# A decoder layer on one core: Silu as one activation, and elementwise work moved from GpSimd to VectorE

## The chip, the cores and the metric

The kernel runs on one core of one Trainium2 chip. A core has a tensor engine (PE in the profile), a vector engine (DVE), a scalar engine (ACT), GpSimd (POOL) and SyncE (SP), which here only starts transfers. Each engine takes its instructions in order and waits on semaphores for what others make. The metric is the device time of one execution in microseconds; lower is better.

## The reference

One decoder layer over 512 tokens of width 1024, in float32:

```python
h = layer_norm(x, ln_in_g, ln_in_b)
proj = h @ w_in
pool_in, qkv, z, beta_raw, a_raw, gate_a, gate_b = split(proj)
y_a = multiscale_pool(pool_in, pool_w, pool_scale)   # trailing means over 2, 4, 8, 16 positions minus the token
y_b = gated_deltanet(qkv, z, beta_raw, a_raw, ...)   # silu(conv4(qkv)), delta rule, rms norm * silu(z)
mixed = sigmoid(gate_a) * y_a + sigmoid(gate_b) * y_b
h = layer_norm(alpha * h + mixed @ w_out, ln1_g, ln1_b)
r = alpha * h + square(relu(h @ w_up)) @ w_down
h = layer_norm(r + sigmoid(r @ ple_gate_w) * (p @ ple_proj_w), ln2_g, ln2_b)
```

The convolution is causal over 4 positions, one filter per channel, and silu(a) is a * sigmoid(a).

## The kernel before, in words

Activations are kept with features on the 128 partitions and the 512 tokens along the row. A wide product runs as three float32r passes over exact splits of both operands: `hi` holds the upper bits, `lo` the rest (`three`, L66 to L68). A weight comes in slabs of 128 x 1024 numbers: SP requests `raw`, ScalarE casts `hi` (L57), VectorE subtracts to get `lo` (L58). There are three `raw` buffers and four of each half, so a slab's cast waits until TensorE has left an older slab.

Start (L146 to L254): SP requests eight halves of x rows, then six rows of parameters into `prow` (L154, L155), then 16 columns for beta and decay, the first two slabs of the weight of k (`raw_k`, L188) and some small rows. VectorE takes statistics, GpSimd makes scale and offset, ScalarE normalises (L219), TensorE transposes into `ps_in`, ScalarE applies gain and offset to get `hf_in` (L239), and VectorE (for two blocks of eight ScalarE) makes the high part of `act` (L240), VectorE the low one (L241). The first two slabs are split in `k0_part`: VectorE casts `hi`, GpSimd subtracts `lo` in two halves (L202). TensorE runs the small product `ps_ba` and the first tile of k, block by block, as `act` comes.

Front, solver and scan (L380 to L600), four pairs of heads: for each of k, q and v of a head a product into PSUM, then `conv`: ScalarE scales the tile into `acc` (L350), VectorE adds three shifted multiples (L352), ScalarE takes the sigmoid into `sg` (L355), GpSimd multiplies (L356). The decay matrices `E` are made beside the first pair: VectorE and GpSimd multiply masks (`gs`, L320), TensorE sums them into `ps_d`, ScalarE takes the exponential (L327), GpSimd clears a triangle (L328). A solver and a scan over the chunks follow, with many small products between those of the next pair.

Trailing means (L633 to L650): TensorE makes a tile, ScalarE copies it, GpSimd adds shifted copies, one to four times for the four windows, ten in all (L640).

Gates (L676 to L720), four rounds of two tiles: `ps_z` with a sigmoid and a product on VectorE (L685) into `zs`; `ps_gb` with a sigmoid `sgb` (L692) and two products on GpSimd, by `sgb` (L693) and by the delta rule's output `onT` (L694); `ps_ga` with a sigmoid `sga` (L710), which VectorE multiplies by the lifted means (L714) and GpSimd adds to `zs` (L716); ScalarE and VectorE split the sum into `mx` (L718, L719). Between them VectorE makes the residual rows `y` (L668 to L671). In the output projection (L754 to L756) TensorE goes through four banks `ps_wo` in turn; the third one becomes free when the last `sga` has been multiplied. The feed-forward part and the last norm follow.

The order on each engine is set by a scheduler that works from modelled times when the program is built; `high_priority` puts the weight splits ahead.

## Time and profile before

| | |
|---|---|
| median of three runs | 887.84 us (886.15 to 889.31) |
| span of the profiled execution | 886.5 us; its device time is not given apart from the three runs |
| TensorE, matmuls | busy 860.3 us, 97% |
| TensorE, weight loads, beside the matmuls | 715.3 us, 81% |
| VectorE | 521.7 us, 59% |
| ScalarE | 357.5 us, 40% |
| GpSimd | 151.6 us, 17% |

The shares are means over stages with different limits, so the page is followed by views of single stretches: what TensorE waited for, busy time by stretch with the granted clock, and the instructions of an engine in order of time. In a row of the last kind the first number is the start and the second the duration; what is in brackets at its end is idle time before it and what ended that.

### The profile page before, as it was taken

What the parts mean: (1) busy time and instruction counts of PE and PEld (TensorE: products, weight loads), DVE (VectorE), ACT (ScalarE), POOL (GpSimd) and SP (SyncE); (2) the same over time, 40 slices, a digit from 0 to 9 for tenths busy, and PEclk for the clock granted to TensorE, in tenths of its full rate; (3) what the DMA queues carried; (4) which work ended last, traced back from release to release, by engine and by line L of the source; (5) the groups of instructions that cost most, each with busy time, mean ns of one, the idle gap of its engine ahead of it and who ended that gap; (6) DMA issues with size and microseconds to landing.
All of it is one profiled execution on the core that took longest, in us unless ns stands there. A gap on an engine that the chain in (4) does not pass through costs nothing.

```text
span 886.5 us, 12477 instructions
## 1 busy us (share of the span) xinstructions
PE 860.3 (97%) x4944; PEld 715.3 (81%) x4944; DVE 521.7 (59%) x991; ACT 357.5 (40%) x567; POOL 151.6 (17%) x135
## 2 busy tenths in 40 slices
PE   7999999999999999998999999999999999999994
PEld 5777888888888888886888888888888888888883
DVE  8898988769759336368366544433344443333456
ACT  4566455365544535333136444322124442222311
POOL 6182312113403031324000000000000000000034
PEclk9999999999999999999999999999999999999997
DMA  6322222222211313183215333333323323233202
GB/s 196 96 59 85 72 73 80 65 72 72 78 50 53 97 31 97 52 283 96 72 32 182 96 95 95 119 96 95 95 85 103 99 95 96 95 96 95 95 10 86
DMA packets 72427, 80.63 MB, mean 91 GB/s; under 512 B 4009, under 2 KB 64818, under 8 KB 72370
## 3 DMA queue, kind: packets, MB, share of 16 engines
q1 hardware_dynamic: 72370, 79.85, 29.6%
q8 instruction: 39, 0.64, 0.3%
q14 instruction: 18, 0.15, 0.1%
HBM read 77.74 MB, written 2.10 MB: 90 GB/s over the span
## 4 chain that ended last, share of the span: by engine, by line
PE 89%; DVE 6%; ACT 2%; POOL 1%; issue 1%; DMA 1%; SPq 0%; POOLq 0%; ACTq 0%; DVEq 0%
PE ps_dn L67 7%; PE ps_dn L68 7%; PE ps_dn L66 7%; PE ps_up L67 6%; PE ps_up L68 6%; PE ps_up L66 6%; PE ps_z L67 2%; PE ps_z L68 2%; PE ps_gb L66 2%; PE ps_gb L68 2%; PE ps_v L67 2%; PE ps_z L66 2%; PE ps_gb L67 2%; PE ps_v L68 2%; PE ps_v L66 2%; PE ps_ga L66 2%
## 5 line engine op out<-in xcount | busy, mean ns | idle before, releaser
L67 PE MATMUL ps_dn<-hid,hi_dn 128*128 128x512 f32 x256 | 99.9, 390 | 0.0
L68 PE MATMUL ps_dn<-hid,lo_dn 128*128 128x512 f32 x256 | 99.9, 390 | 0.0
L66 PE MATMUL ps_dn<-hid,hi_dn 128*128 128x512 f32 x256 | 99.7, 389 | 0.0
L58 DVE TENSOR_TENSOR lo_dn<-raw_dn,hi_dn 128x1024 fp32r<-128x1024 f32 x32 | 39.2, 1225 | 82.9 <-ACT hi_dn L57 82.9
L57 ACT CAST hi_dn<-raw_dn 128x1024 fp32r<-128x1024 f32 x32 | 33.7, 1054 | 96.8 <-PE ps_dn L67 85.2
L887 POOL TENSOR_TENSOR y<-y,rp 128x512 f32<-128x512 f32 x4 | 6.3, 1613 | 380.5 <-PE ps_pg L756 380.5
L66 PEld LDWEIGHTS ps_dn<-hid,hi_dn 128*128 128x128 f32 x256 | 48.1, 188 | 10.0
L67 PEld LDWEIGHTS ps_dn<-hid,hi_dn 128*128 128x128 f32 x256 | 48.1, 188 | 10.0
L68 PEld LDWEIGHTS ps_dn<-hid,lo_dn 128*128 128x128 f32 x256 | 48.1, 188 | 9.7
L849 DVE TENSOR_TENSOR relu<-relu 128x512 f32<-128x512 f32 x32 | 22.2, 693 | 53.3 <-ACT hid L848 53.3
L846 ACT ACTIVATE relu<-ps_up 128x512 f32<-128x512 f32 x32 | 19.0, 595 | 55.8 <-PE ps_up L68 55.8
L693 POOL TENSOR_TENSOR zs<-zs,sgb 128x512 f32<-128x512 f32 x8 | 15.0, 1875 | 88.0 <-ACT sgb L692 88.0
L850 DVE TENSOR_TENSOR hid<-relu,hid 128x512 fp32r<-128x512 f32 x32 | 22.1, 691 | 1.1
L352 DVE SCALAR_TENSOR_TENSOR acc_q<-ps_q,ccol,acc_q 128x511 f32<-128x511 f32 (+2 forms) x24 | 17.8, 742 | 6.3 <-ACT acc_q L350 6.0
L848 ACT ACTIVATE hid<-relu 128x512 fp32r<-128x512 f32 x32 | 20.3, 633 | 1.0
L451 DVE TENSOR_TENSOR sh<-sh,ya 128x120 f32<-128x120 f32 (+14 forms) x60 | 19.4, 324 | 0.7
L356 POOL TENSOR_TENSOR kq<-acc_k,sg_k 128x512 f32<-128x512 f32 x8 | 10.9, 1366 | 48.9 <-ACT sg_k L355 48.9
L58 DVE TENSOR_TENSOR lo_pg<-raw_pg,hi_pg 128x1024 fp32r<-128x1024 f32 x8 | 9.6, 1222 | 16.3 <-ACT hi_pg L57 16.3
L121 ACT ACTIVATE hf_l<-ps_l,pcol 128x128 f32<-128x128 f32 x32 | 11.9, 472 | 17.1 <-PE ps_l L116 17.1
L557 ACT ACTIVATE vn<-ps_s,cc 128x128 f32<-128x128 f32 x32 | 11.1, 367 | 18.6 <-PE ps_s L555 18.5
L352 DVE SCALAR_TENSOR_TENSOR acc_k<-ps_k,ccol,acc_k 128x511 f32<-128x511 f32 (+2 forms) x24 | 17.8, 742 | 1.3 <-ACT acc_k L350 1.2
L58 DVE TENSOR_TENSOR lo_wo<-raw_wo,hi_wo 128x1024 fp32r<-128x1024 f32 x8 | 10.8, 1354 | 13.0 <-ACT hi_wo L57 13.0
(947 smaller groups left out, 2557.0 us busy)
## 6 DMA issues: line engine op xcount, KB each, us to landing
raw_dn<-in_w_down_dram SPq DMA_DIRECT2D x32, 512.0 KB, 3.5
raw_wo<-in_w_out_dram SPq DMA_DIRECT2D x8, 512.0 KB, 4.0
raw_pg<-in_ple_gate_w_dram SPq DMA_DIRECT2D x8, 512.0 KB, 3.6
x<-in_x_dram SPq DMA_DIRECT2D x8, 256.0 KB, 5.3
y<-in_x_dram SPq DMA_DIRECT2D x4, 512.0 KB, 9.3
out_dram<-y SPq DMA_DIRECT2D x7, 256.0 KB, 2.0
raw_k<-in_w_in_dram SPq DMA_DIRECT2D x2, 512.0 KB, 4.0
raw_pp<-in_ple_proj_w_dram SPq DMA_DIRECT2D x2, 512.0 KB
```

The lines of the kernel that those rows point to most:

```text
L57: A.copy(hi, raw)
L58: V.tensor_tensor(out=lo, in0=raw, in1=hi.bitcast(F32), op=SUB)
L66: T.matmul(ps, wh, ah, start=first, stop=False)
L67: T.matmul(ps, wh, al, start=False, stop=False)
L68: T.matmul(ps, wl, ah, start=False, stop=last)
L352: marks[name + "v"] = V.scalar_tensor_tensor(out=acc[:, s:], in0=ps[:, :SEQ - s], scalar=w(3 - s), in1=acc[:, s:], op0=MULT, op1=ADD)
L451: V.tensor_tensor(out=sh[:, :, :m], in0=sh[:, :, :m], in1=ya[:, :, k:k + 1].to_broadcast([P, U8, m]), op=MULT)
L693: G.tensor_tensor(out=zs[m], in0=zs[m], in1=sg, op=MULT)
L846: A.activation(r, ps, AF.Relu)
L848: A.activation(hl[:, 0, :], r, AF.Square)
L849: V.tensor_tensor(out=r, in0=r, in1=r, op=MULT)
L850: V.tensor_tensor(out=hl[:, 1, :], in0=r, in1=hl[:, 0, :].bitcast(F32), op=SUB)
```

## The change

Five edits:

- The six parameter rows are requested by ScalarE's queue instead of SP's.
- The first two slabs: VectorE subtracts `lo`, in one instruction of 128 x 1024; `hi` of the second is cast by ScalarE, and the second split is issued behind block 2 instead of block 1.
- `conv` ends in one Silu activation; the sigmoid tile and GpSimd's product go (24 times).
- The ten adds of the trailing means go from GpSimd to VectorE.
- The 16 gate products and the eight sums go from GpSimd to VectorE; the product by `onT` now comes ahead of the one by `sgb`.

Comments and empty lines are changed too, so later line numbers are one to three lower.

```diff
     for i, v in enumerate((ln_in_g, ln_in_b, ln1_g[0], ln1_b[0], pool_scale[0])):
-        dma(out=prow[8 * i:8 * i + 8, :], in_=v.rearrange("(a b) -> a b", b=P))
-    dma(out=prow[40:41, :], in_=o_norm_w)
+        A.dma_start(out=prow[8 * i:8 * i + 8, :], in_=v.rearrange("(a b) -> a b", b=P))
+    A.dma_start(out=prow[40:41, :], in_=o_norm_w)
...
-        V.tensor_copy(hi, raw)
-        for a in range(0, 4, 2):
-            G.tensor_tensor(out=lo[:, a:a + 2, :], in0=raw[:, a:a + 2, :], in1=hi[:, a:a + 2, :].bitcast(F32), op=SUB)
+        (A.copy if i else V.tensor_copy)(hi, raw)
+        V.tensor_tensor(out=lo, in0=raw, in1=hi.bitcast(F32), op=SUB)
         return hi, lo
...
-        if kb == 1:
+        if kb == 2:
             with tc.issue_after(vec_last.ins):
                 wk0.append(k0_part(1))
...
-        sg = tpa.tile([P, SEQ], F32, tag="sg", bufs=2, name=f"sg_{name}")
-        A.activation(sg, acc, AF.Sigmoid)
-        G.tensor_tensor(out=dst, in0=acc, in1=sg, op=MULT)
+        A.activation(dst, acc, AF.Silu)
...
             for _ in range(g + 1):
-                G.tensor_tensor(out=dst[:, PAD:], in0=src[:, PAD:], in1=src[:, PAD - sh:PAD + SEQ - sh], op=ADD)
+                V.tensor_tensor(out=dst[:, PAD:], in0=src[:, PAD:], in1=src[:, PAD - sh:PAD + SEQ - sh], op=ADD)
...
-            G.tensor_tensor(out=zs[m], in0=zs[m], in1=sg, op=MULT)
-            G.tensor_tensor(out=zs[m], in0=zs[m], in1=onTs[o], op=MULT)
+            V.tensor_tensor(out=zs[m], in0=zs[m], in1=onTs[o], op=MULT)
+            V.tensor_tensor(out=zs[m], in0=zs[m], in1=sg, op=MULT)
...
-            G.tensor_tensor(out=ya, in0=ya, in1=sg, op=ADD)
+            V.tensor_tensor(out=ya, in0=ya, in1=sg, op=ADD)
```

The order on VectorE at the start, from the last statistics on; `hi_k` and `lo_k` are the two parts of the first slabs, `hf_in` and `act` the blocks of the normalised input. Before:

```order
L103 BN_AGGR mv_in<-st_in_181 128x2
L221 TENSOR_SCALAR x_115<-x_115,mv_in,rstd_in 128x512
L227 CAST hi_ba<-raw_ba 128x8x16
L200 CAST hi_k_196<-raw_k_144 128x1024
L240 CAST act<-hf_in_206 128x512
L241 TENSOR_TENSOR act<-hf_in_206,act 128x512
L240 CAST act<-hf_in_215 128x512
L241 TENSOR_TENSOR act<-hf_in_215,act 128x512
L200 CAST hi_k_219<-raw_k_146 128x1024
```

After:

```order
L103 BN_AGGR mv_in<-st_in_181 128x2
L220 TENSOR_SCALAR x_115<-x_115,mv_in,rstd_in 128x512
L226 CAST hi_ba<-raw_ba 128x8x16
L200 CAST hi_k_196<-raw_k_144 128x1024
L201 TENSOR_TENSOR lo_k_197<-raw_k_144,hi_k_196 128x1024
L239 CAST act<-hf_in_205 128x512
L240 TENSOR_TENSOR act<-hf_in_205,act 128x512
L239 CAST act<-hf_in_214 128x512
L240 TENSOR_TENSOR act<-hf_in_214,act 128x512
```

The low part of the first slab now stands on VectorE between its cast and the first block of `act`; the cast of the second slab has gone to ScalarE.

The order on VectorE ahead of the output projection, up to the last `sga`, with `y` the residual rows and `lo_wo` the low parts of the output weight's slabs; `zs_4045` and `zs_4074` are the two gate tiles before, `zs_3995` and `zs_4024` the same after. Before:

```order
L671 TENSOR_TENSOR y_3762<-y_3762,gb_in 128x1024
L670 TENSOR_TENSOR y_4240<-y_4240,gb_in 128x1024
L58 TENSOR_TENSOR lo_wo_4270<-raw_wo_4267,hi_wo_4269 128x1024
L671 TENSOR_TENSOR y_4001<-y_4001,gb_in 128x1024
L671 TENSOR_TENSOR y_4240<-y_4240,gb_in 128x1024
L58 TENSOR_TENSOR lo_wo_4276<-raw_wo_4273,hi_wo_4275 128x1024
L714 SCALAR_TENSOR_TENSOR sga_4193<-ps_lift_4195,pcol,sga_4193 128x512
L58 TENSOR_TENSOR lo_wo_4282<-raw_wo_4279,hi_wo_4281 128x1024
L719 TENSOR_TENSOR mx_4201<-zs_4045,mx_4201 128x512
L58 TENSOR_TENSOR lo_wo_4288<-raw_wo_4285,hi_wo_4287 128x1024
L714 SCALAR_TENSOR_TENSOR sga_4229<-ps_lift_4231,pcol,sga_4229 128x512
```

After:

```order
L58 TENSOR_TENSOR lo_wo_4220<-raw_wo_4217,hi_wo_4219 128x1024
L667 TENSOR_TENSOR y_4190<-y_4190,gb_in 128x1024
L668 TENSOR_TENSOR y_3951<-y_3951,gb_in 128x1024
L58 TENSOR_TENSOR lo_wo_4226<-raw_wo_4223,hi_wo_4225 128x1024
L691 TENSOR_TENSOR zs_4024<-zs_4024,sgb_4092 128x512
L668 TENSOR_TENSOR y_4190<-y_4190,gb_in 128x1024
L711 SCALAR_TENSOR_TENSOR sga_4143<-ps_lift_4145,pcol,sga_4143 128x512
L713 TENSOR_TENSOR zs_3995<-zs_3995,sga_4143 128x512
L58 TENSOR_TENSOR lo_wo_4232<-raw_wo_4229,hi_wo_4231 128x1024
L716 TENSOR_TENSOR mx_4151<-zs_3995,mx_4151 128x512
L58 TENSOR_TENSOR lo_wo_4238<-raw_wo_4235,hi_wo_4237 128x1024
L711 SCALAR_TENSOR_TENSOR sga_4179<-ps_lift_4181,pcol,sga_4179 128x512
```

One gate product and one sum now stand among VectorE's rows here; three products more stand a little earlier. The slabs of the output weight and the two `sga` keep their order among each other.

The order on ScalarE there, after; it is the same as before but for line and buffer numbers:

```order
L689 ACTIVATE sgb_4092<-ps_gb_4067 128x512
L707 ACTIVATE sga_4143<-ps_ga_4118 128x512
L57 CAST hi_wo_4231<-raw_wo_4229 128x1024
L715 CAST mx_4151<-zs_3995 128x512
L57 CAST hi_wo_4237<-raw_wo_4235 128x1024
L707 ACTIVATE sga_4179<-ps_ga_4154 128x512
```

ScalarE thus casts the sum of the sixth tile (`mx`) ahead of the fourth slab, and that one ahead of the last `sga`. Table loads on ScalarE: ten rows before, eleven after, where the one more stands at the first sigmoid of the gates (L680).

## Rows read from the trace of the kernel before

**Rows 1.** The page's first part: busy time, share of the span and instructions of each engine.

```profile
PE 860.3 (97%) x4944; PEld 715.3 (81%) x4944; DVE 521.7 (59%) x991; ACT 357.5 (40%) x567; POOL 151.6 (17%) x135
```

**Rows 2.** What TensorE waited for: total us, times, longest.

```profile
PE ps_wo L754 <- DVE sga L714: 3.5, 1, 3.5
...
PE ps_d L325 <- ACT E L327: 1.5, 1, 1.5
...
PE ps_q L66 <- DVE acc_k L352: 1.5, 2, 1.0
```

**Rows 3.** Stretches: their length, busy us of each engine with its instructions, then TensorE's granted clock, the share of the transfer engines and GB/s.

```profile
60.00:70.00 10.00, 8.47 (x39) 6.59 (x39) 9.95 (x15) 7.49 (x10) 6.84 (x7) 1.00 0.31 83
...
200.00:250.00 50.00, 50.00 (x420) 41.88 (x418) 39.37 (x127) 25.21 (x49) 17.05 (x15) 1.00 0.23 67
...
300.00:350.00 50.00, 50.00 (x335) 42.66 (x334) 23.60 (x46) 22.84 (x46) 11.15 (x8) 1.00 0.23 67
...
410.00:420.00 10.00, 6.50 (x30) 5.11 (x29) 6.98 (x10) 3.93 (x7) 3.50 (x2) 0.93 0.58 188
```

**Rows 4.** GpSimd's first split and VectorE's rows beside it, in order of time.

```profile
14.22 2.68 POOL L202 TENSOR_TENSOR lo_k<-raw_k,hi_k 128x512 fp32r<-128x512 f32 x2 [1.43 <-DVE hi_k L200]
...
13.45 0.69 DVE L200 CAST hi_k<-raw_k 128x1024 fp32r<-128x1024 f32 x1 [1.20 <-DMA raw_k<-in_w_in_dram]
14.30 1.47 DVE L240 CAST act<-hf_in 128x512 fp32r<-128x512 f32 x1 [0.16 <-ACT hf_in L239]
...
17.37 0.41 DVE L240 CAST act<-hf_in 128x512 fp32r<-128x512 f32 x1
```

**Rows 5.** TensorE in the same stretch: its first product, the last of the five that work on the first block, and one later wait.

```profile
15.92 0.60 PE L253 MATMUL ps_ba<-act,hi_ba 128*32 128x512 f32 x1 [0.94 <-DVE act L240]
...
18.45 0.63 PE L68 MATMUL ps_k<-act,lo_k 128*128 128x512 f32 x1
...
23.24 0.42 PE L254 MATMUL ps_ba<-act,hi_ba 128*32 128x512 f32 x1 [0.32 <-DVE act L241]
```

**Rows 6.** The requests of the start: the page's line for x (KB each, median us to landing), SP's queue for the first parameter row and the first slabs (start, duration), and ScalarE's first instruction.

```profile
x<-in_x_dram SPq DMA_DIRECT2D x8, 256.0 KB, 5.3
...
4.55 0.51 SPq L154 DMA_DIRECT2D prow<-in_ln_in_g_dram  x1
...
9.46 0.94 SPq L188 DMA_DIRECT2D raw_k<-in_w_in_dram  x2
...
5.65 1.28 ACT L219 ACT_TABLE_LOAD   x1 [5.65 <-DMA prow<-in_ln_in_b_dram]
```

**Rows 7.** VectorE and GpSimd between 56 and 68 us, in order of time for each.

```profile
57.14 1.25 DVE L397 TENSOR_SCALAR ssk<-ssk 128x8 f32<-128x8 f32 x1
...
59.74 0.17 DVE L400 TENSOR_SCALAR ncc<-cc 128x8 f32<-128x8 f32 x1
...
62.97 1.22 DVE L58 TENSOR_TENSOR lo_k1b<-raw_k1b,hi_k1b 128x1024 fp32r<-128x1024 f32 x1
...
65.22 2.29 DVE L58 TENSOR_TENSOR lo_q1a<-raw_q1a,hi_q1a 128x1024 fp32r<-128x1024 f32 x1
...
56.88 1.49 POOL L356 TENSOR_TENSOR kq<-acc_q,sg_q 128x512 f32<-128x512 f32 x1 [0.20 <-ACT sg_q L355]
...
61.29 1.04 POOL L320 TENSOR_TENSOR gs<-upper,glo 128x512 fp32r<-128x512 f32 x1
...
65.13 1.29 POOL L356 TENSOR_TENSOR vT<-acc_v,sg_v 128x512 f32<-128x512 f32 x1 [2.22 <-ACT sg_v L355]
```

**Rows 8.** Around the start of the output projection, in order of time for each of TensorE, ScalarE and VectorE.

```profile
411.53 0.39 PE L67 MATMUL ps_ga<-act,hi_ga3b 128*128 128x512 f32 x1
...
414.02 0.40 PE L756 MATMUL ps_wo<-hi_wo,mx 128*128 128x512 f32 x1
417.92 0.50 PE L754 MATMUL ps_wo<-hi_wo,mx 128*128 128x512 f32 x1 [3.50 <-DVE sga L714]
...
422.14 0.39 PE L756 MATMUL ps_wo<-hi_wo,mx 128*128 128x512 f32 x1
422.36 0.39 PE L754 MATMUL ps_wo<-hi_wo,mx 128*128 128x512 f32 x1
...
409.24 1.05 ACT L57 CAST hi_wo<-raw_wo 128x1024 fp32r<-128x1024 f32 x1 [1.84 <-PE ps_ga L67]
414.38 0.62 ACT L718 CAST mx<-zs 128x512 fp32r<-128x512 f32 x1 [4.09 <-POOL zs L716]
414.91 1.04 ACT L57 CAST hi_wo<-raw_wo 128x1024 fp32r<-128x1024 f32 x1
...
398.37 1.79 DVE L668 TENSOR_SCALAR y<-y,mv_in,rstd_in 128x1024 f32<-128x1024 f32 x1
...
405.68 2.31 DVE L58 TENSOR_TENSOR lo_wo<-raw_wo,hi_wo 128x1024 fp32r<-128x1024 f32 x1
```

**Rows 9.** Groups by line, engine and shape: busy us, mean ns of one | idle time of the engine before them, and what ended most of it.

```profile
L693 POOL TENSOR_TENSOR zs<-zs,sgb 128x512 f32<-128x512 f32 x8 | 15.0, 1875 | 88.0 <-ACT sgb L692 88.0
...
L640 POOL TENSOR_TENSOR pads<-pads 128x512 f32<-128x512 f32 x10 | 10.9, 1085 | 19.0 <-ACT pads L638 14.2 <-DVE sh L451 4.3
...
L849 DVE TENSOR_TENSOR relu<-relu 128x512 f32<-128x512 f32 x32 | 22.2, 693 | 53.3 <-ACT hid L848 53.3
...
L355 ACT ACTIVATE sg_v<-acc_v 128x512 f32<-128x512 f32 x8 | 5.1, 632 | 13.2 <-DVE acc_v L352 7.6 <-DVE ya L453 5.6
```

## The prediction

> **What bounds the kernel now.** I read the shares of busy time first: TensorE is busy for 860.3 of 886.5 us, VectorE for 521.7, ScalarE for 357.5, GpSimd for 151.6 [rows 1]. So an edit gains only where it takes idle or slow time from TensorE, about 26 us in all, part of it at the kernel's end, which the change leaves alone. The second view is the list of what TensorE waited for [rows 2]. One entry is large, 3.5 us for the vector engine's scaled gate `sga` at the first bank of the output projection; then come 1.5 us for the scalar engine's `E` and twice together 1.5 us for the vector engine's `acc_k`. Third, the stretches [rows 3]: in 60 to 70 us TensorE has 8.47 of 10 while VectorE has 9.95, and in 410 to 420 it has 6.50 at a granted clock of 0.93. Between 200 and 350 us TensorE is never idle, while VectorE has 39.4 and 23.6 of 50. So three places can gain: the start, 60 to 90 us, and the start of the output projection. Everywhere else the question is only whether the work that VectorE gets stays hidden.
>
> **The start.** The first half of `k`'s weight is split by GpSimd from 14.22 us for 2.68 us, and beside it VectorE's first cast of `act` takes 1.47 us; the next such cast takes 0.41 [rows 4]. TensorE's first product waits for that cast, 0.94 us, and starts at 15.92 [rows 5]. In the changed order VectorE splits this half itself ahead of the casts (1.22 us by the same form at 62.97 [rows 7]). That fits: the weight is now requested right behind x and not behind six parameter rows, which put SP's request at 9.46 instead of about 5 [rows 6], and VectorE stands idle for 1.20 us until 13.45, waiting for this weight [rows 4]. The first cast then ends at 14.30 + 0.41 = 14.71 instead of 15.77, and TensorE starts 1.06 us earlier. The wait of 0.32 us at 23.24 [rows 5] is also one for `act`, and the casts behind it come earlier by the stretch of the second split; I take it as gone: 1.38 us. The cast of the weight's second half goes to ScalarE, between blocks 0 and 1 of `act`: 1.05 us there (the same shape at 409.24 [rows 8]). Block 1 is later by that, but TensorE first has five products of block 0, which took it from 15.92 to 18.45 [rows 5], so I cost it at nothing; without that cover it is 1.05.
>
> Bounds: the early products run at the lower of two clock levels, 0.60 to 0.63 us, five of them up to 18.45 [rows 5], against 0.39 later [rows 8]; if the earlier start brings the upper level for all, that is 5 x 0.24 = 1.2 more, 2.6 in all. On the other side the weight's 1 MB now moves while the last x are in flight. These land 5.3 us after requests that end at about 4.5, so at 9.8 [rows 6]; if weight and x shared the transfer engines evenly from 5.0 on, the last x would be up to half of 4.8 us late, and the term would be -1.0. I take 1.38, the value nearest to the rows, because the requests stand in one queue behind x. The Trainium skill, "DMA: Bandwidth & Descriptors", section "Issuing engines are not separate DMA queues", says that transfers started by different engines run on the same 16 engines and interleave, and that a second issuer saves only issue time. By that rule the parameter rows gain nothing by coming from ScalarE and could at worst mix with x, which for 20 KB is nothing; the 0.51 us of an issue [rows 6] is what moves. Six issues of at most that on ScalarE end before its table load at 5.65, so they cost nothing; if they took twice that, from about 0.8 us on, they would push the first normalisation of x by about 1 us.
>
> **60 to 90 us.** The wait at `ps_d` hangs on `E`, which ScalarE computes behind a table load and the sigmoid of `acc_v`, which hangs on VectorE. VectorE is full there, and two of its instructions are stretched beside GpSimd's product `acc`*`sg`: L397 takes 1.25 us where an instruction of the same shape takes 0.17, and `lo_q1a` 2.29 where `lo_k1b` takes 1.22 [rows 7]. Without these products the chain is shorter by 1.08 + 1.07 = 2.15 us, of the 2.99 that TensorE waits there: 1.08 off the wait for `E`, the rest off the two for `acc_k`. I take 2.15. The upper bound is 2.99. The lower one is nothing: GpSimd's masks L320 stay, move up when the products go, and stop VectorE elsewhere, each 1.04 us long [rows 7]. The Trainium skill, "SBUF — State Buffer", section "Who interferes with whom", has a rule for this: a VectorE instruction with two SBUF inputs and a GpSimd one that reads SBUF exclude each other, and whichever comes second waits for the whole of the first. The trace agrees: L397 ends at 58.39, the GpSimd product at 58.37. By that rule two masks that get in the way would take 2.08 back, and the whole sum would be 6.1 instead of 8.2, about 881.8 us.
>
> Silu itself is not in the trace. It replaces a sigmoid of 0.63 us [rows 9]; if it took twice as long, the result would still come earlier, since a GpSimd product of 1.29 to 1.49 us [rows 7] is left out behind it. Table loads stay as many up to 90 us, and one is added at the first output gate: 1.28 us [rows 6] on an engine with 22.8 busy of 50 [rows 3], beside a TensorE that has 24 products of 0.23, 5.5 us, for the next bank. I cost it at nothing.
>
> **The output projection.** TensorE's third bank could follow the product of 414.02 at 414.25; it follows at 417.92, and from there on to 422.36 twelve steps take 4.44 us instead of 12 x 0.23 = 2.76, at the lower clock [rows 8]: 3.67 + 1.68 = 5.35 us lost. The last `sga` was late since ScalarE cast the fourth weight slab only at 414.91, behind the cast of a sum that GpSimd delivered late, and VectorE's rows before it were stretched beside GpSimd's gate products: four of them from 398.37 to 405.68, each about 1.05 us (2.31 where 1.22 is usual) [rows 7, 8]. With the products and sums on VectorE these 4.2 us go, against four products and one sum at 0.69 [rows 9], 3.5 us. What is late next is the slab's buffer: the third slab's cast began at 409.24, as TensorE left the previous slab; for the fourth this is the end of the product at 411.53, so 411.92 + 0.04. From there the old distance of 414.91 to 417.92 holds, 3.01 us, and TensorE starts at 414.97: 2.95 us earlier, with a wait of 0.7. After the wait of 1.53 us at 67 us the stretch shows a clock of 1.00 [rows 3], so I count the slow steps as gone as well: 2.95 + 1.68 = 4.63. Bounds: 5.35, and 0 if VectorE's added instructions keep the last `sga` where it was.
>
> **The rest.** Ten adds of the means and the 24 gate instructions bring VectorE 34 x 0.69 = 23.5 us between 205 and 418 us [rows 9]. I cost them at nothing beyond the above, for TensorE has work there throughout and VectorE's share stays under 0.93 in 200 to 250 us ((39.4 + 6.9)/50) [rows 3].
>
> **Sum.** 1.38 + 2.15 + 4.63 = 8.16 us off the profiled execution's span of 886.5, so 878.3. The median of the runs is 1.3 us above that span; 887.84 - 8.16 = 879.7 us.
>
> **Rivals.** First, the last `sga` stays late, because VectorE, now alone with rows of y, splits and gates, is the bound in 392 to 418 us. For it: what it is given there, 3.5 us, is nearly what it is spared, 4.2. Against it: the fourth slab's cast needs only TensorE and the sum before it, and that sum no longer waits for GpSimd. Then 1.38 + 2.15 = 3.5 us are left: 884.3.
>
> Second, the change does not do what it says: the stretched instructions are lengthened by something that stays, the masks and the transfers of y, and the earlier casts are limited by `hf_in`. For it: GpSimd keeps its masks in the very stretch where VectorE is full. Against it: the ends that coincide to 0.02 us. Then 0 to 2 us: about 887.
>
> Third, slower. VectorE takes its instructions in order. A gate product waits there for ScalarE's sigmoid, which waits for a full bank; GpSimd stood 88 us before these eight products [rows 9], where nobody was behind it. Behind it on VectorE stand the next weight's low parts and the scan's state updates, for which TensorE waits. If half of the 23.5 us shows up on TensorE, 11.7 - 8.2 = 3.6 us are lost: 891.4; all of it would be 903. It decides from a third on, 8.2 of 23.5. Against it: TensorE is never idle in the two stretches between 200 and 350 us now [rows 3], and in the changed order the splits of a slab stand well ahead of its products.
>
> **How the numbers follow.** Forecast 0.62, late `sga` 0.14, no effect 0.12, slower 0.12. A difference under 0.3%, 2.7 us, can't be told from no change. The first two cases are faster: 0.76; the third is the same: 0.12; the fourth slower: 0.12. With all upper bounds, 2.6 + 2.99 + 5.35 = 10.9, the time is 876.9; an unseen gain of the same kind puts the low end at 875.5. The high end, 886.5, takes in the late `sga` and the better part of no effect and leaves out the slower case.
>
> **What would show it.** Right: the first `act` cast at about 0.41 us and TensorE's first product near 14.9; L397 under 0.3 us and the wait for `E` under 0.6; in the output projection a wait for `sga` under 1 us and a clock of 1.00; TensorE without waits between 200 and 350 us. Wrong: waits for `act` or x at the start longer than now, the `ps_wo` wait still at 3 us, or new waits of TensorE for `S`, `rr` or `lo` between 200 and 400 us.

## The result and the profile after

The changed kernel takes 881.25 us (median of four runs, 880.27 to 881.79) against 887.31 us for the kernel before, run beside it (886.15 to 889.31): 6.06 us less by these medians. The ratio on record is 0.9923 with a 95% interval of 0.9904 to 0.9942 (the quotient of the two medians, 0.9932, lies in it), which is 6.8 us less, between 5.1 and 8.5. The prediction had 8.16 less and 879.7. The profiled execution has a span of 879.4 us, 7.1 under that of before.

The page's first part, as in [rows 1]:

```profile
PE 858.7 (98%) x4944; PEld 715.1 (81%) x4944; DVE 516.4 (59%) x1026; ACT 361.1 (41%) x569; POOL 63.1 (7%) x73
```

GpSimd has lost 88.5 us of its 151.6, and VectorE, with 35 instructions more, is busy for 5 us less: its stretched instructions are mostly gone. TensorE's busy time falls by only 1.6 us, so most of the gain is idle time. What TensorE waited for, as in [rows 2] (total us, times, longest), with the one entry above these:

```profile
PE ps_in L233 <- ACT x L218: 3.3, 4, 1.6
...
PE ps_d L324 <- ACT E L326: 0.7, 1, 0.7
...
PE ps_q L66 <- DVE acc_k L351: 0.5, 1, 0.5
```

The entry for `ps_wo` is gone; the wait for ScalarE's normalised x at the start has grown from 2.5 to 3.3 us. The same stretches as in [rows 3]: length, busy us of each engine with its instructions, TensorE's granted clock, the share of the transfer engines, GB/s.

```profile
60.00:70.00 10.00, 9.32 (x44) 7.47 (x43) 9.51 (x16) 7.25 (x10) 3.71 (x6) 1.00 0.36 105
...
200.00:250.00 50.00, 50.00 (x400) 42.11 (x399) 40.23 (x128) 26.07 (x48) 4.52 (x3) 1.00 0.24 67
...
300.00:350.00 50.00, 50.00 (x286) 42.52 (x285) 25.18 (x50) 22.08 (x42) 2.01 (x2) 1.00 0.23 67
...
410.00:420.00 10.00, 10.00 (x49) 8.13 (x48) 5.95 (x8) 4.18 (x6) 0.00 (x0) 1.00 0.30 105
```

To see where the time went, the starts of the same TensorE products were compared, kernel after minus kernel before, as a median over each stretch. The table gives what each stage adds to that difference, worked out from the profiled executions; negative is a gain. It holds all kernels run, so that the experiments can refer to it. The column "in all" is the difference from 450 us on, and the sum of those before it.

Each row rests on one execution of its kernel and on one of before, and executions of one program differ: those of before lie between 885.83 and 890.03 us, those of silu_back, means_back and order_only spread by 2.3 to 3.4 us, those of gates_back by 0.3. The profiled execution is 1.2 us above the median for silu_back and 2.5 above for means_back, and 1.6 below it for order_only, so the stages of these three rows are less firm than their decimals look.

| kernel | up to 30 us | wait at 67 us | wait at 80 us | 95 to 395 us | output projection | in all | median us | ratio, interval |
|---|---|---|---|---|---|---|---|---|
| after | -0.78 | -0.85 | -0.74 | +0.48 | -5.21 | -7.11 | 881.25 | 0.9923 [0.9904, 0.9942] |
| gates_back | -1.60 | -0.85 | -0.77 | -0.27 | -5.21 | -8.71 | 879.38 | 0.9901 [0.9885, 0.9917] |
| sums_back | -0.66 | -0.87 | -0.76 | +0.83 | -5.23 | -6.69 | 881.18 | 0.9922 [0.9900, 0.9944] |
| products_back | -1.51 | -0.85 | -0.78 | +0.11 | -5.22 | -8.25 | 880.19 | 0.9913 [0.9891, 0.9934] |
| silu_back | -1.07 | -0.01 | +0.02 | +1.80 | -1.28 | -0.54 | 886.71 | 0.9982 [0.9969, 0.9995] |
| means_back | +1.33 | -0.84 | -0.73 | +2.55 | -3.53 | -1.23 | 884.46 | 0.9960 [0.9945, 0.9974] |
| prow_sp | -2.46 | -0.85 | -0.74 | +0.48 | -5.22 | -8.79 | 879.66 | 0.9904 [0.9887, 0.9920] |
| prow_late | -0.01 | -0.85 | -0.77 | +0.51 | -5.23 | -6.34 | 882.14 | 0.9932 [0.9908, 0.9956] |
| split_back | -0.11 | -0.85 | -0.77 | +0.51 | -5.22 | -6.45 | 882.09 | 0.9934 [0.9909, 0.9960] |
| order_only | -0.11 | 0.00 | -0.80 | 0.00 | -4.55 | -5.46 | 884.66 | 0.9962 [0.9948, 0.9976] |
| gates_alone | +0.49 | -0.01 | -0.02 | +1.72 | -4.55 | -2.36 | 885.90 | 0.9969 [0.9959, 0.9979] |
| gates_back_old | +0.68 | -0.85 | -0.78 | -0.27 | -3.73 | -4.95 | 882.30 | 0.9934 [0.9919, 0.9948] |
| best | -1.79 | -0.85 | -0.78 | -0.27 | -5.21 | -8.89 | 879.25 | 0.9898 [0.9884, 0.9913] |

From 420 us to the end no kernel's difference moves by more than 0.02 us.

**The start after.** The requests (start, duration), on SP's queue and then on ScalarE's, VectorE's last statistics of x, and ScalarE's last normalisation of x:

```profile
0.79 5.78 SPq L148 DMA_DIRECT2D x<-in_x_dram  x8
...
7.09 1.75 SPq L188 DMA_DIRECT2D raw_k<-in_w_in_dram  x2
...
0.79 0.58 ACTq L154 DMA_DIRECT2D prow<-in_ln_in_g_dram  x1
...
4.40 0.23 ACTq L155 DMA_DIRECT2D prow<-in_o_norm_w_dram  x1
...
10.30 0.69 DVE L102 BATCH_NORM_STATS2 st_in<-x 128x6 f32<-128x512 f32 x1 [0.40 <-DMA x<-in_x_dram]
...
12.87 0.81 ACT L218 ACTIVATE x<-x,nmr,rstd_in 128x512 f32<-128x512 f32 x1 [1.47 <-POOL nmr L215]
```

The eight requests for x now take 5.78 us. Before they ended by 4.55, where SP's first parameter row begins [rows 6]. VectorE's statistics wait for the last x. VectorE and TensorE behind that:

```profile
13.23 0.78 DVE L200 CAST hi_k<-raw_k 128x1024 fp32r<-128x1024 f32 x1 [0.31 <-DMA raw_k<-in_w_in_dram]
14.04 1.23 DVE L201 TENSOR_TENSOR lo_k<-raw_k,hi_k 128x1024 fp32r<-128x1024 f32 x1
15.19 0.42 DVE L239 CAST act<-hf_in 128x512 fp32r<-128x512 f32 x1
...
15.75 0.60 PE L252 MATMUL ps_ba<-act,hi_ba 128*32 128x512 f32 x1
...
17.43 0.63 PE L68 MATMUL ps_k<-act,lo_k 128*128 128x512 f32 x1
```

The first cast of `act` is as short as forecast, 0.42 us instead of 1.47 [rows 4], but it starts 0.89 us later than in [rows 4]. TensorE's first product gains 0.17 us on [rows 5] and still takes 0.60; its fifth gains 1.02, 17.43 against 18.45.

**55 to 67 us after**, against [rows 7] (VectorE, ScalarE and GpSimd):

```profile
55.59 0.17 DVE L394 TENSOR_SCALAR ssk<-ssk 128x8 f32<-128x8 f32 x1
...
58.90 0.75 DVE L351 SCALAR_TENSOR_TENSOR acc_v<-ps_v,ccol,acc_v 128x511 f32<-128x511 f32 x1 [1.35 <-ACT acc_v L349]
...
61.33 1.47 DVE L58 TENSOR_TENSOR lo_k1b<-raw_k1b,hi_k1b 128x1024 fp32r<-128x1024 f32 x1
...
63.85 1.21 DVE L58 TENSOR_TENSOR lo_q1a<-raw_q1a,hi_q1a 128x1024 fp32r<-128x1024 f32 x1
...
66.34 0.69 DVE L368 TENSOR_REDUCE ssq<-sq_q 128x4 f32<-128x512 f32 x1 [0.35 <-ACT sq_q L367]
...
62.79 0.64 ACT L353 ACTIVATE vT<-acc_v 128x512 f32<-128x512 f32 x1
...
60.10 1.04 POOL L319 TENSOR_TENSOR gs<-upper,glo 128x512 fp32r<-128x512 f32 x1
```

`ssk` takes 0.17 us instead of 1.25 and `lo_q1a` 1.21 instead of 2.29, as forecast. Two things were not: VectorE then waits for ScalarE, 1.35 us for its scaled tile and later 0.35 for `sq_q`, and `lo_k1b` takes 1.47 instead of 1.22 beside GpSimd's work that has moved up.

**The output projection after**, against [rows 8] (ScalarE, VectorE, TensorE):

```profile
407.35 1.05 ACT L57 CAST hi_wo<-raw_wo 128x1024 fp32r<-128x1024 f32 x1 [1.90 <-PE ps_ga L67]
...
410.06 1.05 ACT L57 CAST hi_wo<-raw_wo 128x1024 fp32r<-128x1024 f32 x1 [1.15 <-PE ps_ga L67]
...
412.29 0.75 DVE L711 SCALAR_TENSOR_TENSOR sga<-ps_lift,pcol,sga 128x512 f32<-128x512 f32 x1
...
412.35 0.39 PE L751 MATMUL ps_wo<-hi_wo,mx 128*128 128x512 f32 x1
...
413.09 0.50 PE L751 MATMUL ps_wo<-hi_wo,mx 128*128 128x512 f32 x1
```

The fourth slab's cast now waits only for TensorE. The row of 412.35 is the third bank's first product, which follows without a wait; the fourth bank's, at 413.09, stands right behind the last `sga`. Steps of 0.23 us and a clock of 1.00 follow.

### The profile page after: what moved, and what is told of

Read it like the earlier page. It is cut to its first block, busy times and chain, and to the rows that moved or that the text cites. A ratio compares the mean times of both kernels' runs of the same rounds, so it can differ in the third digit from the quotient of the medians.

```text
span 879.4 us, 12396 instructions
## 1 busy us (share of the span) xinstructions
PE 858.7 (98%) x4944; PEld 715.1 (81%) x4944; DVE 516.4 (59%) x1026; ACT 361.1 (41%) x569; POOL 63.1 (7%) x73
## 4 chain that ended last, share of the span: by engine, by line
PE 89%; DVE 5%; ACT 3%; POOL 1%; issue 1%; DMA 1%; SPq 0%; POOLq 0%; ACTq 0%; DVEq 0%
PE ps_dn L66 7%; PE ps_dn L68 7%; PE ps_dn L67 7%; PE ps_up L67 7%; PE ps_up L68 7%; PE ps_up L66 7%; PE ps_z L68 2%; PE ps_gb L67 2%; PE ps_ga L68 2%; PE ps_z L67 2%; PE ps_gb L68 2%; PE ps_gb L66 2%; PE ps_z L66 2%; PE ps_ga L67 2%; PE ps_ga L66 2%; PE ps_q L66 1%
## 5 line engine op out<-in xcount | busy, mean ns | idle before, releaser
L576 POOL TENSOR_TENSOR rs<-rs,mhalf 128x4 f32<-128x4 f32 x8 | 9.4, 1173 | 162.8 <-DVE rs L575 162.8
L351 DVE SCALAR_TENSOR_TENSOR acc_v<-ps_v,ccol,acc_v 128x511 f32<-128x511 f32 (+2 forms) x24 | 17.8, 742 | 2.6 <-ACT acc_v L349 2.5
L883 DVE TENSOR_TENSOR y<-y,pproj 128x512 f32<-128x512 f32 (+1 forms) x9 | 9.2, 1035 | 14.9 <-ACT y L881 14.9
L57 ACT CAST hi_wo<-raw_wo 128x1024 fp32r<-128x1024 f32 x8 | 8.4, 1053 | 23.1 <-PE ps_wo L753 15.1
```

What stands on the lines that cost most here:

```text
L57: A.copy(hi, raw)
L351: marks[name + "v"] = V.scalar_tensor_tensor(out=acc[:, s:], in0=ps[:, :SEQ - s], scalar=w(3 - s), in1=acc[:, s:], op0=MULT, op1=ADD)
```

## Experiments

All edits are made on the changed kernel unless said otherwise, each kernel beside before on the same chip. The theory tested first is the prediction's: each part gains what was forecast for it, and the gates gain because GpSimd no longer does them. Its rival is that something else in the new program, the order of the instructions or who is stretched by whom, did it. Each expectation names what it tells apart.

**1. Gates back on GpSimd, in the new order.**

```diff
-            V.tensor_tensor(out=zs[m], in0=zs[m], in1=onTs[o], op=MULT)
-            V.tensor_tensor(out=zs[m], in0=zs[m], in1=sg, op=MULT)
+            G.tensor_tensor(out=zs[m], in0=zs[m], in1=onTs[o], op=MULT)
+            G.tensor_tensor(out=zs[m], in0=zs[m], in1=sg, op=MULT)
...
-            V.tensor_tensor(out=ya, in0=ya, in1=sg, op=ADD)
+            G.tensor_tensor(out=ya, in0=ya, in1=sg, op=ADD)
```

> The changed kernel with its 16 gate products and eight sums on GpSimd again; all else as changed. Theory (the gates moved to VectorE gave the 5.2 us that the two traces show around 412 us): TensorE's wait at ps_wo of about 3.5 us and the slow steps behind it return, the span is about 5 us over the changed kernel's 879.4, near 884.5, and the offset against the kernel before is unchanged up to 400 us. Rival (the gain came with the bank that waits, which is the fourth in the changed program and the third before): the wait is at most 3 us and the span under 882.

Measured: 879.38 us (879.19 to 879.47), ratio 0.9901, not slower than the changed kernel, whose interval overlaps; the gain at the output projection is the same 5.21 us. The prediction's reason for its largest term falls: the 24 instructions need not leave GpSimd. GpSimd's rows ahead of the projection, and the last of VectorE's rows beside the first of them whose inputs both lie outside PSUM:

```profile
399.27 6.53 POOL L691 TENSOR_TENSOR zs<-zs,sgb 128x512 f32<-128x512 f32 x1 [6.23 <-ACT sgb L689]
405.76 1.30 POOL L713 TENSOR_TENSOR zs<-zs,sga 128x512 f32<-128x512 f32 x1
...
403.44 1.21 DVE L668 TENSOR_TENSOR y<-y,gb_in 128x1024 f32<-128x1024 f32 x1
```

This time GpSimd's product is the one that is held, 6.53 us where 1.30 is usual, while VectorE's rows beside it have their usual 1.21; it ends 1.15 us after the last of these. VectorE has lost about 1 us twice before, at 389 and 391 us. Nothing but the sum stands behind it, and that is in time.

**2. Only the eight sums, or only the 16 products, back on GpSimd** (the last line of the diff above, or the first two).

> The changed kernel with only the eight sums of the gates on GpSimd again. Theory A (the last sga was late because ScalarE's cast of the sum waited for GpSimd): a wait at ps_wo of 1 to 2 us returns, since the sum takes 1.3 us or more there instead of 0.7; span 880.5 to 882. Theory B (it was late because VectorE was stretched beside the products): no wait over 0.3 us, span 879.4.

> The changed kernel with only the 16 gate products on GpSimd again. Theory B (VectorE's rows of y and the splits are stretched beside them, about 4 us from 395 to 408): the stretches return, and with them a wait at ps_wo of 2 to 3.5 us; span 882 to 884. Theory A: no wait over 0.5 us, span 879.4.

Measured: 881.18 and 880.19 us; neither shows a wait at `ps_wo`, and they keep 5.23 and 5.22 us there, so each of the two theories above fails in one of the two runs. Neither half of the move is needed for the gain.

**3. The order of the two products alone, on the kernel before.** The products stay on GpSimd; that with `onT` goes first.

```diff
-            G.tensor_tensor(out=zs[m], in0=zs[m], in1=sg, op=MULT)
             G.tensor_tensor(out=zs[m], in0=zs[m], in1=onTs[o], op=MULT)
+            G.tensor_tensor(out=zs[m], in0=zs[m], in1=sg, op=MULT)
```

> The kernel before with one edit: GpSimd multiplies zs by onT first and by sgb second, so that the first product runs early and only one stands behind the sigmoid. Theory (the last sga was late because two GpSimd products in a row met VectorE's rows of y and stretched them by 4.2 us): the stretches halve, TensorE's wait at ps_wo falls from 3.5 to about 1 us, the slow steps behind it go as they did where the wait was 1.1, span near 882. Rival (the place of the products does not matter, only the engine): wait 3.5 us, span 886.5.

Measured: 884.66 us, ratio 0.9962. TensorE's order is that of before, and 4.55 of the 5.21 us at the projection are there with nothing moved between engines. By the ratio the swap is worth 3.4 us in all (2.1 to 4.6); the profiled execution, the fastest of five, has 5.46, of which 0.80 come from the wait at 80 us, which the swap doesn't touch. GpSimd's product and the third bank's first:

```profile
401.86 6.96 POOL L694 TENSOR_TENSOR zs<-zs,sgb 128x512 f32<-128x512 f32 x1 [5.09 <-ACT sgb L692]
...
414.07 0.50 PE L754 MATMUL ps_wo<-hi_wo,mx 128*128 128x512 f32 x1 [0.56 <-DVE sga L714]
```

The wait is 0.56 us instead of 3.50 [rows 8], the slow steps are gone, and again it is GpSimd that is held here. Two of VectorE's rows, at 394 and 396 us, lose about 1 us each, where four did before.

**4. The old order on the changed kernel, gates on GpSimd.** As experiment 1, with the product by `sgb` first.

> The changed kernel with all 24 gate instructions on GpSimd, the two products in the old order, by sgb first. Theory (the order of the products matters, not the engine): where the same kernel with the new order has no wait and a span of 877.7, a wait at ps_wo of 2 to 3.5 us returns, stretches of about 4 us on VectorE's rows of y stand ahead of it, and the span is 880.5 to 883. Rival (something else of the new program, the bank that waits or when the rows of y start, removed the wait): no wait, span near 878.

Measured: 882.30 us. The projection gains 3.73 us where experiment 1 gains 5.21: with the order of all other instructions the same, the swap is worth 1.48 us there. GpSimd:

```profile
401.48 6.59 POOL L690 TENSOR_TENSOR zs<-zs,sgb 128x512 f32<-128x512 f32 x1 [4.32 <-ACT sgb L689]
408.14 1.30 POOL L691 TENSOR_TENSOR zs<-zs,onT 128x512 f32<-128x512 f32 x1
409.39 2.27 POOL L713 TENSOR_TENSOR zs<-zs,sga 128x512 f32<-128x512 f32 x1
```

The second product stands behind the held one and pushes the sum, which is itself stretched to 2.27 us, to 409.39, 3.6 us later than in experiment 1, of which 2.3 us is what this kernel is behind as a whole by then. ScalarE's cast of the sum, and with it the last slab and the last `sga`, follow; TensorE waits 1.4 us.

**5. Gates alone on VectorE, on the kernel before** (the four other parts stay as they were).

```diff
-            G.tensor_tensor(out=zs[m], in0=zs[m], in1=sg, op=MULT)
-            G.tensor_tensor(out=zs[m], in0=zs[m], in1=onTs[o], op=MULT)
+            V.tensor_tensor(out=zs[m], in0=zs[m], in1=onTs[o], op=MULT)
+            V.tensor_tensor(out=zs[m], in0=zs[m], in1=sg, op=MULT)
...
-            G.tensor_tensor(out=ya, in0=ya, in1=sg, op=ADD)
+            V.tensor_tensor(out=ya, in0=ya, in1=sg, op=ADD)
```

> The kernel before with the gates' 24 instructions on VectorE, by onT first, and nothing else changed. If the move does what the prediction said, the wait at ps_wo is 0.7 to 1.1 us at the third bank, without slow steps, and about 4.5 us are gained: span near 882, offset before 380 us near 0. If the program's other edits are needed for it, the wait stays at 2 us or more.

Measured: 885.90 us. The projection gains 4.55 us, just what the swap alone gains, and 1.72 us are lost between 95 and 395 us. So on the old kernel the move to VectorE adds nothing to the swap.

**6. Sigmoid and product back in place of Silu.**

```diff
-        A.activation(dst, acc, AF.Silu)
+        sg = tpa.tile([P, SEQ], F32, tag="sg", bufs=2, name=f"sg_{name}")
+        A.activation(sg, acc, AF.Sigmoid)
+        G.tensor_tensor(out=dst, in0=acc, in1=sg, op=MULT)
```

> The changed kernel with the sigmoid and GpSimd's product in place of Silu. Theory (Silu's gain is that VectorE is no longer stretched beside these products at 56 to 66 us): the offset against the kernel before is -0.8 from 30 to 60 us and stays near -0.8 behind 90 us where the changed kernel has -2.4; span about 881. Rival (the stretches move to other instructions, or the gain is from the result being earlier): the stretch of L394 or of a low part returns without a longer wait for E, and the offset behind 90 us is under -2.

Measured: 886.71 us. Both waits of 60 to 90 us are back to within 0.02 us, and so are the stretches (`ssk` takes 1.25 us again, `lo_q1a` 2.29), so that term belongs to Silu. But the span is 886.0 and not near 881: against the changed kernel 1.3 us are lost in the middle and 3.9 at the projection, where this edit touches nothing. Of the ten runs five lie at 885.0 to 885.8 us and five at 887.6 to 888.4; the profile is one of the latter, so the 3.9 may be less in others. What TensorE waited for:

```profile
PE ps_wo L753 <- DVE sga L713: 2.2, 1, 2.2
PE ps_d L324 <- ACT E L326: 1.5, 1, 1.5
PE ps_q L66 <- DVE acc_k L351: 1.5, 2, 0.9
```

VectorE and TensorE:

```profile
404.66 0.81 DVE L667 TENSOR_SCALAR y<-y,mv_in,rstd_in 128x1024 f32<-128x1024 f32 x1
...
413.54 0.48 PE L753 MATMUL ps_wo<-hi_wo,mx 128*128 128x512 f32 x1
```

With other costs the scheduler has made another program: the rows of `y` begin at 404.66, 8.9 us ahead of the first output product, where in the changed kernel the first stands at 390.56, 20 us ahead. VectorE is the bound there, with no gate on GpSimd and no stretched row. That is the prediction's first rival, in another program than the one it was set up for.

**7. Trailing means back on GpSimd.**

```diff
-                V.tensor_tensor(out=dst[:, PAD:], in0=src[:, PAD:], in1=src[:, PAD - sh:PAD + SEQ - sh], op=ADD)
+                G.tensor_tensor(out=dst[:, PAD:], in0=src[:, PAD:], in1=src[:, PAD - sh:PAD + SEQ - sh], op=ADD)
```

> The changed kernel with the ten adds of the means on GpSimd again. Theory (the 0.5 us that the changed kernel loses between 100 and 380 us comes from VectorE's added work, the adds among the solver's and the scan's steps): the offset at 380 us is -2.2 to -2.5 instead of -1.9 and the span 878.9 to 879.2. Rival (the gate products cause the loss, or the order of TensorE's products): offset -1.9, span 879.4.

Measured: 884.46 us, 3 us slower than the changed kernel though VectorE has ten instructions less; neither of the outcomes named above came. In the profiled execution, the slowest of seven, the loss is 5.9 us and stands in three places that the ten adds don't touch: the start (2.1 us against after), the middle (2.1) and the projection (1.7, with a wait of 1.1 us at the third bank). The start is read in experiment 8; the middle and the projection are again another interleaving.

**8. The parameter rows on SP again, between x and the weights.**

```diff
-        A.dma_start(out=prow[8 * i:8 * i + 8, :], in_=v.rearrange("(a b) -> a b", b=P))
-    A.dma_start(out=prow[40:41, :], in_=o_norm_w)
+        dma(out=prow[8 * i:8 * i + 8, :], in_=v.rearrange("(a b) -> a b", b=P))
+    dma(out=prow[40:41, :], in_=o_norm_w)
```

> The changed kernel with the six parameter rows requested by SP again, between x and the first weights. Theory (the requests from ScalarE ran beside SP's requests of x, which took 5.78 us instead of 3.71, so the last x came late): SP's eight requests take 3.7 us again, VectorE's two waits of 0.4 us for x go, the last ScalarE instruction L218 starts near 12.2 instead of 12.87; but the first weight lands near 13.4, so its split ends near 15.3 and the first cast of act at about 15.7. TensorE's first product then stands near 15.9 instead of 15.75, offset at 30 us about -0.6 instead of -0.8. Rival (x is late because the weights' 1 MB shares the transfer engines with it): the requests still take over 5 us or x is still waited for.

Measured: 879.66 us; the start gains 2.46 us instead of 0.78, and every later stage is that of the changed kernel to 0.01. SP's x, the last normalisation and the first product:

```profile
0.79 3.71 SPq L148 DMA_DIRECT2D x<-in_x_dram  x8
...
12.35 0.81 ACT L218 ACTIVATE x<-x,nmr,rstd_in 128x512 f32<-128x512 f32 x1 [0.42 <-POOL nmr L215]
...
15.89 0.39 PE L252 MATMUL ps_ba<-act,hi_ba 128*32 128x512 f32 x1
```

The requests for x take 3.71 us again, as in all six programs whose rows SP requests, before among them (3.71 or 3.72); in the eight programs in which ScalarE requests beside them they take 5.39 to 6.05. So ScalarE's requests stretch SP's. The second thing is the clock: the first product comes no earlier than before, but at 0.39 us and not at 0.60. The windows of 16 to 18 us, their columns those of the stretches above, first of prow_sp:

```profile
16.00:18.00 2.00, 2.00 (x12) 1.47 (x12) 2.00 (x5) 2.00 (x4) 0.00 (x0) 1.00 0.73 191
```

The same of the changed kernel, and behind it of gates_back and of means_back, which all have the same start in the code:

```profile
16.00:18.00 2.00, 2.00 (x6) 1.21 (x6) 1.53 (x4) 2.00 (x4) 0.00 (x0) 0.50 0.92 266
```

gates_back:

```profile
16.00:18.00 2.00, 1.99 (x11) 1.34 (x11) 1.56 (x4) 2.00 (x4) 0.00 (x0) 1.00 0.84 234
```

means_back:

```profile
16.00:18.00 2.00, 1.31 (x5) 0.61 (x4) 1.78 (x4) 1.97 (x3) 0.00 (x0) 0.50 0.59 156
```

A granted clock of 1.00 is the level of 2.4 GHz, 0.50 that of 1.2. gates_back stays at the upper level and gains 1.60 us, the changed kernel is at the lower one here and back at 1.00 from 19 us and gains 0.78, means_back is still at the lower one up to 21 us and loses 1.33. So the start of one and the same code varies by 3 us between these programs, and a difference of under 1 us there is settled by no single profile. The level granted goes with it, but isn't all: products_back is at the lower level between 14 and 17 us and gains 1.51, and in means_back x is requested for longest, 6.05 us. Between the two that stay at the upper level, prow_sp and gates_back, 0.86 us are left for the requests. What decides the level wasn't found: up to 14 us these four have 1.00.

**9. The parameter rows on SP behind the weights.** The six requests are moved as they are behind the two of `raw_k`.

> The changed kernel with the six parameter rows requested by SP behind the first weights, so that nothing is requested beside x and the weights come early. Theory (ScalarE's requests slow SP's): SP's requests of x take 3.7 us, VectorE does not wait for x, the weight lands by about 10.5, and TensorE's first product stands near 15.0, offset at 30 us about -1.4 instead of -0.8. Rival (the weights' bytes slow x): x is waited for as in the changed kernel, 0.8 us in all, and the offset stays -0.8.

Measured: 882.14 us, with nothing gained at the start; the expectation fails. x is in time here too, but the rows are not. SP's requests of the weights, TensorE's product that makes the columns, and ScalarE's copy of them:

```profile
5.22 2.32 SPq L185 DMA_DIRECT2D raw_k<-in_w_in_dram  x2
...
14.40 0.22 PE L223 MATMUL ps_prow<-ident,prow 41*128 41x41 f32 x1 [0.51 <-DMA prow<-in_pool_scale_dram]
...
14.66 0.19 ACT L224 COPY pcol<-ps_prow 128x41 f32<-128x41 f32 x1 [0.34 <-PE ps_prow L223]
```

The columns stand ready at 14.85, in the changed kernel at 13.76, and `hf_in` needs them. The rows are small, but they have to be there first.

**10. The first weight split as before.** VectorE casts both slabs, GpSimd subtracts in halves, and the second split is behind block 1.

```diff
-        (A.copy if i else V.tensor_copy)(hi, raw)
-        V.tensor_tensor(out=lo, in0=raw, in1=hi.bitcast(F32), op=SUB)
+        V.tensor_copy(hi, raw)
+        for a in range(0, 4, 2):
+            G.tensor_tensor(out=lo[:, a:a + 2, :], in0=raw[:, a:a + 2, :], in1=hi[:, a:a + 2, :].bitcast(F32), op=SUB)
...
-        if kb == 2:
+        if kb == 1:
```

> The changed kernel with the first weight split as before, casts on VectorE and the subtraction on GpSimd. Theory (beside GpSimd's split the casts of act are stretched): the first cast of act takes over 1.3 us again and TensorE's first product stands near 16.4, 0.7 later than in the changed kernel; offset at 30 us near 0 instead of -0.8. Rival (the early weight lets the split end before the casts, so they are not stretched): the cast takes 0.4 us, offset -0.8.

Measured: 882.09 us; the start's gain goes (-0.11 against -0.78) and all else stays. VectorE's first two rows on `act`:

```profile
14.93 0.66 DVE L240 CAST act<-hf_in 128x512 fp32r<-128x512 f32 x1 [0.96 <-ACT hf_in L239]
15.62 1.65 DVE L241 TENSOR_TENSOR act<-hf_in,act 128x512 fp32r<-128x512 f32 x1
```

The loss is not where it was expected: the first cast takes 0.66 us and not over 1.3, and TensorE's first product stands at 15.74, as in the changed kernel. It is the low part behind the cast that is stretched, to 1.65 us where 0.69 is usual, and a wait of 0.7 us for `act` comes back at `ps_ba`. The 0.67 us lie within what the start varies by.

**11. Both findings together:** gates on GpSimd in the new order, parameter rows on SP.

> The changed kernel with the gates on GpSimd (new order) and the parameter rows requested by SP between x and the weights. If the parts add up as the offsets of the single runs say, -2.4 at the start, -1.7 up to 90 us, about -0.3 in the middle, -5.2 at the output projection: span near 877, time near 878.5, faster than both kernels. If the start depends on when the x rows land, the span is 877 to 879.

Measured: 879.25 us, ratio 0.9898 with 0.9884 to 0.9913. It beats the kernel before. All its runs (at most 879.35) lie below all of the changed kernel's (at least 880.27), but the two intervals overlap, and against gates_back (879.38) and prow_sp (879.66) the runs can't tell. The start gains 1.79 us, not 2.46, at the upper clock level throughout. ScalarE's second normalisation waits longer, and the first product is later:

```profile
9.80 2.63 ACT L218 ACTIVATE x<-x,nmr,rstd_in 128x1024 f32<-128x1024 f32 x2 [1.34 <-DMA prow<-in_ln_b_dram]
...
16.52 0.40 PE L252 MATMUL ps_ba<-act,hi_ba 128*32 128x512 f32 x1 [0.22 <-DVE act L239]
```

So the 0.86 us from experiment 8 are no firm price either.

## Why the prediction was right, and where it was not

The forecast of faster and the range held: 881.25 in 875.5 to 886.5, 1.6 us from the value named. It is right in its three places; of its reasons two fell, those of the start and of the output projection, and the term of 60 to 90 us was mis-sized. That the total came so near is in part luck: three shortfalls, 0.60 at the start, 0.56 at 60 to 90 us and 0.48 in the middle, stand against a surplus of 0.58 at the projection.

**The start: forecast 1.38, measured 0.78.** The failed step is "six issues of at most that on ScalarE end before its table load at 5.65, so they cost nothing", with the assumption that "the requests stand in one queue behind x". It priced the requests on ScalarE's own time only. Beside them SP's requests for x became 2.07 us longer (5.78 against 3.71), ScalarE's last normalisation 0.67 later (12.87 against 12.20), and the first cast of `act` with it; the other 0.22 of its 0.89 us is VectorE's `lo_k` in front of it, since the weight, requested at 7.09 and not at about 5, landed only for 13.23. The shortened cast, 1.05 us, was right and paid for this. Two of the prediction's own signs of being wrong are here: the first product stands at 15.75 and not near 14.9, and TensorE waits longer for x than before, 3.3 us for 2.5. The upper bound, 2.6 for the upper clock level from the first product on, is near the 2.46 of prow_sp, but not by the bound's working: there the level is the upper one, while the first product comes no earlier than before. The Trainium skill, "DMA: Bandwidth & Descriptors", section "Issuing engines are not separate DMA queues", says that a second issuing engine saves only the time it takes to issue. The traces go further than that: here it took SP's time as well.

**60 to 90 us: forecast 2.15, measured 1.59** (0.85 + 0.74). The mechanism is shown: the two named instructions fell from 1.25 to 0.17 and from 2.29 to 1.21, and with the sigmoid and the product back both waits return. The term of 1.08 us for `E` measured 0.85, since VectorE then waits for ScalarE, and that of 1.07 for `acc_k` measured 0.74: VectorE waits for ScalarE once more, 0.35 us for `sq_q`, and of TensorE's two waits for `acc_k` only the first goes, the second is 0.55 us instead of 0.51. The wait for `E` is 0.68 us, over the 0.6 that was named. A second witness for the term of `acc_k` is order_only, whose instructions are those of before here; VectorE and GpSimd:

```profile
65.12 1.22 DVE L58 TENSOR_TENSOR lo_q1a<-raw_q1a,hi_q1a 128x1024 fp32r<-128x1024 f32 x1
...
65.04 3.05 POOL L356 TENSOR_TENSOR vT<-acc_v,sg_v 128x512 f32<-128x512 f32 x1 [2.23 <-ACT sg_v L355]
```

In [rows 7] the same two instructions take 2.29 and 1.29. So 0.80 us hang on which engine loses: where it is GpSimd, the wait at 80 us falls from 0.95 to 0.17. The masks that were feared to take 2.08 us back took nothing that shows: the 0.25 us that `lo_k1b` lost beside GpSimd in the changed kernel are not lost in order_only, and the gain at 80 us is about the same, 0.74 and 0.80. One reading of the prediction is off: L397 has a single tile as its input, so its end beside that of GpSimd's product is no case of the rule for two inputs; `lo_q1a`, which has two, is one.

**The output projection: forecast 4.63, measured 5.21.** The times were right to a hundredth: the fourth slab's cast was to start at 411.96 and TensorE 3.01 us behind it at 414.97; less the 1.89 us that the kernel was ahead by then, this is 410.07 and 413.08, and the trace has 410.06 and 413.09. What was mis-sized is "with a wait of 0.7": in the changed program the bank that the last `sga` frees is the fourth, not the third, so TensorE has three products more, 0.69 us, to work on meanwhile. The slow steps went as counted. What fell is the reason. Neither the move of the products nor that of the sums is needed (experiments 1 and 2), the swap of two products alone brings 4.55 us there on the old kernel, in one execution (3), and the move adds nothing to it there (5). The swap's own mechanism, one product less behind `sgb` and so ahead of the sum, is worth 1.48 us where all other orders are equal (4). The rest of the 4.55 goes with who is held: in before four of VectorE's rows lost 1.05 us each, in order_only two do, and GpSimd loses 5.7 us in one product (experiment 3). Whether the swap decided that is open; at 65 us it fell one way and the other in two executions of the same instructions.

**The middle: forecast nothing, measured +0.48.** No new wait stands in TensorE's list, so the third rival, products on VectorE that hold up the scan, did not come: it would have shown as waits for `S`, `rr` or `lo`. The shift goes instead with the scheduler's interleaving. Counted in the traces, TensorE changes from wide products to small ones between 95 and 395 us, in the programs with Silu, 69 to 71 times where the column has -0.27 to +0.11, 72 times at +0.48 and +0.51, 74 at +0.83 (sums_back) and 76 at +2.55 (means_back); in those without, 75 times at 0.00 (before, order_only) and 79 at +1.72 and +1.80 (gates_alone, silu_back). That is a correlation within each family of programs and not a tested cause; why after loses 0.48 stays open.

The step that costs most to get wrong was never a term of the sum: any edit changes the program elsewhere. In the profiled executions, going back on Silu cost 3.9 us at the projection, on the means 3.8 us in two stages.

## What to carry to other kernels

When a request moves to another engine's queue, price it also on the queue that is requesting at the same moment, and see which transfer the first work waits for. Before elementwise work is moved off a slow engine, look at what stands behind the instruction that waits there: putting the product whose operands are ready ahead of the one that waits moved no work at all, and here got 4.55 of the 5.21 us that came with the move at that place. Where a scheduler sets the order, compare kernels stage by stage over matched instructions; totals mix an edit's own gain with up to 4 us from the order of work that the edit doesn't touch.

## What was not expected of the hardware

Six requests of ScalarE's queue lengthened eight of SP's from 3.71 us to between 5.39 and 6.05, in eight programs out of eight.

A GpSimd product of 1.30 us took 6.5 to 7.0 us while VectorE's rows ran without a gap (gates_back, gates_back_old, order_only): 5.2 to 5.7 us more, over several instructions of the other engine, where VectorE lost about 1 us at a time. In all three it ended 1.15 to 1.17 us after the last of those rows whose inputs both lie outside PSUM, as if it had begun its 1.30 us only as that row ended. The Trainium skill, "SBUF — State Buffer", section "Who interferes with whom", says that the order of issue decides who blocks. These rows can't confirm it: in before and in order_only the trace lets GpSimd start first at 65 us, by 0.09 and 0.08 us, and in the one VectorE was stretched and in the other GpSimd.

TensorE's slow steps behind a wait at the projection (a granted clock of 0.75 and 0.67 from 417 to 420 us) came with waits of 3.5 and 2.2 us, in before and silu_back, and not with 0.6, 1.1 or 1.4, where the clock stayed at 1.00.
